# A decoder layer on one core: experts taken in order of their load, the emptier half multiplied in two passes

## The chip, the cores and the metric

The program runs on one core of a Trainium2 chip. The metric is the device time of one execution in microseconds (us), from the first to the last instruction on that core and what the runtime puts around it. Lower is better.

## What is computed

One layer of a decoder trunk on 512 tokens of 1024 channels in float32: three parallel token mixers (dilated attention, gated linear attention, sparse attention), merged and projected; then cross-attention into a memory of 256 tokens; then a mixture of 32 experts, four for each token. Each sublayer ends in `LN(alpha * x + y)`. The change touches the mixture alone:

```python
logits = t @ w_router + b_router                       # t: 512 x 1024
top_logits, top_idx = lax.top_k(logits, TOP_K)         # 4 of 32
gates = jax.nn.softmax(top_logits)
...
gu = xb @ w_gu[e] + b_gu[e]                            # 1024 -> 2048, rows xb of expert e
gate = jnp.minimum(gu[:, :D_FF], 7.0)
up = jnp.clip(gu[:, D_FF:], -7.0, 7.0)
y = ((up + 1.0) * gate * jax.nn.sigmoid(1.702 * gate)) @ w_down[e] + b_down[e]
```

Every expert has 3 x 1024 x 1024 float32 weights, 12.6 MB; all 32 are 402.7 MB. 2048 (token, expert) pairs are spread over 32 experts, 64 each in the mean. With the reference's own inputs the router gives the experts between 46 and 90 tokens; experts 0 and 1 have 70 and 49; of the other 30, in order of load, the first fourteen have 90 to 62 and the last sixteen 61 to 46.

## The kernel before

The mixers and the cross-attention take the first half of the span. Products are made in split precision: a float32 operand is written as hi + lo (`hilo`, lines 82 to 85: ACT rounds hi to float32r, DVE subtracts lo = src - hi), and a product is the sum of three float32r products, hi hi + lo hi + hi lo.

Routing (`route_tile`, `route`) puts each token's place in its expert's list into `posm`, its row number and gate into `V`, and the number of tokens of each expert into `cnt`. `slots` (four experts at a time) turns these into row numbers `GI` and gates `GT` of 96 slots (`RB`) an expert: DVE compares `iota` with `posm` into `Pe` (line 1146), PE multiplies `Pe` with `V`.

The mixture (`moe`, lines 1220 to 1334) goes through the experts 0 to 31. For each one:

- `gather`: POOL fetches up to 96 rows of x into `xg` by an indirect DMA (line 1337); PE transposes them (line 80), ACT and DVE write hi and lo into `xgT`.
- `gate`, `up`, `down`: each is one `product` of 1024 x 1024 weights. SP loads the weights in four chunks of 1 MB (`mraw`, line 1215; twelve buffers in turn), ACT writes `mhi` (line 84), DVE writes `mlo` (line 85; three buffers of each). PE holds 128 x 96 of X and streams 512 columns of a chunk past it, twelve matmuls a chunk: X hi with `mhi`, X lo with `mhi`, X hi with `mlo` (lines 1233 to 1236). Two short matmuls add the biases from `Be`.
- After `gate`: DVE takes min(g, 7) out of PSUM (line 1253), ACT the tanh (line 1254), DVE (t + 1) g (line 1255).
- After `up`: DVE clamps half a row of u out of PSUM (line 1264) and multiplies, (u + 1) g (line 1265), twice. PE transposes g, and `hT` gets hi and lo as `xgT` does.
- After `down`: ACT scales by the gates (line 1276), POOL adds the rows to `y_scratch` in DRAM by an indirect DMA (line 1342).

The program's order is gate(e+1), down(e), gather(e+2), up(e+1); a scheduler of the framework then fixes the order on every engine when the program is built. Each engine works its own list strictly in order. The last expert's `down_last` goes by halves of its columns, and LN3 (`finish`) follows from SBUF. Experts with over 96 tokens would go through a loop behind the end (`more_blocks`), which is not entered where the counts fit.

```python
for x, y in ((0, hi), (1, hi), (0, lo)):                                  # 1233
    for k in range(2):
        for h in range(2):
            self.mm(P[:, h], X[x][:, a * 2 + k], y[:, k, h * 512:h * 512 + 512], ...)
...
nc.vector.scalar_tensor_tensor(g, t, 1.0, g, op0=ALU.add, op1=ALU.mult)    # 1255
```

Of the kernel before, what the change touches and what calls it, by code (L numbers as in the profile page):

```python
# [36 lines left out]
def const_arrays():  # L37
    """Masks and identities: functions of the shapes alone."""
# [24 lines left out]
class K:  # L63
# [177 lines left out]
    def p0(self):  # L241
        """x -> LN0 -> x0 (spilled) and h^T as hi/lo."""
# [280 lines left out]
    def gla_head(self, h, U, lev, ng, bp, bq):  # L523
# [27 lines left out]
        # within-chunk scores, by halves of ever smaller blocks, so that every exponent is <= 0  # L551
# [24 lines left out]
        # across chunks  # L576
# [216 lines left out]
    def gates_steps(self, br, n, n0=0):  # L793
        """The first 2n gate blocks of a branch, kept for its merge in places that the branches' outputs leave free."""
# [12 lines left out]
    def merge_steps(self, br, w_br, Y):  # L807
        """merged^T += 2 sigmoid(m_g)^T * (w_br^T y^T); Y: pairs (hi, lo) of [128, 2, S]."""
# [26 lines left out]
    def w_halves(self, w_dram, pool):  # L835
        """[1024, 1024] as hi/lo tiles [128, 4, 512], indexed [half][k // 4]."""
# [15 lines left out]
    def proj_ln(self, W, X, R, g, b, after, order, late):  # L852
        """R[i] (residual) <- LN(alpha R[i] + X^T W) g + b, tile by tile; after(i) follows each."""
# [25 lines left out]
    def mix_out(self, x1p, xT):  # L879
        """w_o_mix and LN1: x1 in x1p, its transpose in xT."""  # L880
# [35 lines left out]
    def xattn(self, R, xh, xT, ap, x2_done, before_xo):  # L916
# [11 lines left out]
        for c in range(4):  # L928
            # in float32 itself: the tensor engine has time here, the others have not
# [76 lines left out]
        w = I["w_xo"][0]  # L1006
        W = [[self.chunk(w[a * 512:a * 512 + 512, h * 512:h * 512 + 512], h and a) for a in range(2)] for h in range(2)]
# [212 lines left out]
    def moe(self, wk, xgp):  # L1220
# [91 lines left out]
        def scatter(e, o):  # L1312
            self.scatter_rows(o, self.GI[:, e:e + 1])
# [338 lines left out]
```

## Time and profile before

| what | value |
|---|---|
| median of 3 runs (lowest, highest) | 2460.72 us (2459.5, 2465.01) |
| span of the profiled execution | 2459.6 us; the fastest run is 2459.5 us, so the profiler's execution stands for the runs |
| PE, DVE, ACT, POOL busy over the span | 2347.8, 1875.0, 1381.1, 313.4 us (95, 76, 56, 13%) |
| DMA | 531.04 MB, mean 216 GB/s; 340 to 373 GB/s in most of the mixture's slices |
| mixture | from about 1225 us to the end |

The 40 slices of the page are 61.5 us each; the mixture fills the last twenty. A busy PE is not a PE at its peak, since the matmuls are pipelined; that is why durations below are taken from the distance between instructions where that matters. Idle time of an engine counts only where another engine waits for it.

### The profile page before, as it was taken

To read this page: it belongs to the slowest core of one execution; us is meant where nothing else is said; L and a number is where in the kernel's file an instruction comes from. 1 tells how busy PE (TensorE), PEld (TensorE's weight loads), DVE (VectorE), ACT (ScalarE), POOL (GpSimd) and SP (SyncE) were. 2 spreads that over 40 slices of the span, in tenths; PEclk is the share of its full clock that TensorE was granted. 3 is DMA by queue.
4 is the path that set the end of the run, shared out by engine and by line. 5 is a ranking of instruction groups with operands and counts; after the bars stand their busy time and mean duration, and the time that the engine had idled before them with its cause. 6 is when DMAs were issued, how large, how long until landed. Compare 5 with 4: busy or idle time off the path is not lost. (4 is left out here: it accounts for less than half of the span.)

```text
span 2459.6 us, 30893 instructions
## 1 busy us (share of the span) xinstructions
PE 2347.8 (95%) x11491; PEld 1800.1 (73%) x11491; DVE 1875.0 (76%) x2745; ACT 1381.1 (56%) x1709; POOL 313.4 (13%) x287
## 2 busy tenths in 40 slices
PE   7999899999999998999899999999999999999995
PEld 6778789878877776887767767767676676676663
DVE  6465567446678674636689989989898889999997
ACT  3444434345566663134167767777676776767773
POOL 2000233111000002002110110110101101102002
PEclk9999899999999999999699999999999999999997
DMA  8432222332221204225689999999999999999992
GB/s 258 112 81 77 64 56 74 96 96 69 69 65 39 66 21 157 84 86 158 235 301 359 359 332 359 350 340 366 323 370 326 345 343 346 361 351 373 353 328 87
DMA packets 259931, 531.04 MB, mean 216 GB/s; under 512 B 32185, under 2 KB 145046, under 8 KB 259648
## 3 DMA queue, kind: packets, MB, share of 16 engines
q1 hardware_dynamic: 244720, 487.89, 57.2%
q0 software_dynamic: 13040, 33.73, 5.4%
q10 hardware_dynamic: 2016, 7.41, 0.8%
q8 instruction: 92, 1.51, 0.2%
q14 instruction: 63, 0.52, 0.1%
HBM read 509.98 MB, written 22.02 MB: 216 GB/s over the span
## 5 line engine op out<-in xcount | busy, mean ns | idle before, releaser
L85 DVE TENSOR_TENSOR mlo<-mraw,mhi 128x2048 fp32r<-128x2048 f32 x384 | 874.1, 2286 | 102.8 <-ACT mhi L84 98.5
L84 ACT ACTIVATE mhi<-mraw 128x2048 fp32r<-128x2048 f32 x387 | 734.4, 1916 | 233.2 <-PE pd L77 180.6
L77 PE MATMUL pd<-mhi,xgT 128*96 128x512 f32 x2080 | 531.9, 396 | 2.6 <-ACT mhi L84 2.2
L77 PEld LDWEIGHTS pd<-mhi,xgT 128*96 128x96 f32 x2080 | 334.6, 162 | 145.6 <-ACT mhi L84 2.7
L77 PE MATMUL pd<-hT,whi 128*128 128x512 f32 (+1 forms) x1136 | 299.3, 408 | 9.7 <-DVE qs L318 4.3
L77 PE MATMUL pd<-mlo,xgT 128*96 128x512 f32 x1040 | 285.9, 396 | 0.1
L77 PE MATMUL pd<-mhi,hT 128*96 128x512 f32 x992 | 266.9, 405 | 14.4 <-DVE hT L85 11.8
L77 PEld LDWEIGHTS pd<-hT,whi 128*128 128x128 f32 (+1 forms) x1136 | 214.9, 193 | 59.9 <-issue 3.9
L85 DVE TENSOR_TENSOR wlo<-raw,whi 128x1024 fp32r<-128x1024 f32 (+1 forms) x121 | 155.6, 1288 | 125.8 <-ACT whi L84 57.8
L84 ACT ACTIVATE whi<-raw 128x1024 fp32r<-128x1024 f32 (+1 forms) x121 | 127.3, 1058 | 185.7 <-PE pd L77 145.2
L77 PEld LDWEIGHTS pd<-mlo,xgT 128*96 128x96 f32 x1040 | 165.3, 161 | 73.2 <-DVE mlo L85 4.5
L77 PEld LDWEIGHTS pd<-mhi,hT 128*96 128x96 f32 x992 | 157.2, 165 | 78.4 <-DVE hT L85 13.6
L1337 POOL DMA_INDIRECT xg<-x_scratch,GI x31 | 71.5, 2308 | 676.9 <-PE pt L80 599.9
L77 PE MATMUL pd<-hT,wlo 128*128 128x512 f32 (+1 forms) x568 | 156.7, 401 | 0.0
L77 PE MATMUL pd<-mlo,hT 128*96 128x512 f32 x496 | 141.1, 407 | 0.0
L77 PEld LDWEIGHTS pd<-hT,wlo 128*128 128x128 f32 (+1 forms) x568 | 104.9, 188 | 22.8 <-issue 0.7
L85 DVE TENSOR_TENSOR ptl<-pt,pth 128x512 fp32r<-128x512 f32 (+4 forms) x144 | 84.6, 606 | 42.7 <-ACT pth L84 41.7
L84 ACT ACTIVATE pth<-pt 128x512 fp32r<-128x512 f32 (+4 forms) x144 | 72.4, 527 | 68.6 <-PE pt L80 67.6
L77 PEld LDWEIGHTS pd<-mlo,hT 128*96 128x96 f32 x496 | 80.2, 167 | 33.4 <-DVE mlo L85 1.5
L1342 POOL DMA_INDIRECT y_scratch<-o,GI x32 | 59.4, 1858 | 329.0 <-ACT o L1276 254.6
L739 ACT ACTIVATE cz<-cz,c_mn 128x128 f32<-128x128 f32 (+3 forms) x128 | 71.1, 556 | 50.8 <-DVE c_mn L737 50.0
L737 DVE CUSTOM_DVE_ANT_0 cz<-ps,m_full 128x128 f32<-128x128 f32 (+3 forms) x128 | 59.9, 486 | 42.2 <-PE ps L77 33.3
(402 smaller groups left out, 3320.0 us busy)
## 6 DMA issues: line engine op xcount, KB each, us to landing
mraw<-in_w_gu_dram SPq DMA_DIRECT2D x256, 1024.0 KB, 8.4
mraw<-in_w_down_dram SPq DMA_DIRECT2D x128, 1024.0 KB, 6.8
raw<-in_w_in_dram SPq DMA_DIRECT2D x78, 512.0 KB, 4.1
kd<-kd POOLq DMA_DIRECT2D x20, 256.0 KB, 4.1
raw<-in_w_xk_dram SPq DMA_DIRECT2D x8, 512.0 KB, 10.2
raw<-in_w_in_dram SPq DMA_DIRECT2D x16, 256.0 KB, 3.5
raw<-in_w_br_b_dram SPq DMA_DIRECT2D x8, 512.0 KB, 4.1
raw<-in_w_br_c_dram SPq DMA_DIRECT2D x8, 512.0 KB, 4.5
```

The lines of the kernel that those rows point to most:

```text
L77: self.nc.tensor.matmul(out, l, r, start=start, stop=stop)
L84: self.nc.scalar.activation(hi, src, AF.Copy)
L85: (eng or self.nc.vector).tensor_tensor(lo, src, hi.bitcast(F32), op=ALU.subtract)
L737: nc.vector.tensor_tensor_reduce(z[:, :n], P[:, :n], self.m_full[:, 512 - n:], -0.125, 1e30, op0=ALU.add, op1=ALU.min, accum_out=mn[:, h, ...
L739: nc.scalar.activation(z[:, :n], z[:, :n], AF.Exp, bias=mn[:, h, k - 1:k], scale=-1.0, accum_out=den[:, h, k - 1:k])
L1337: self.nc.gpsimd.indirect_dma_start(out=xg, out_offset=None, in_=self.x2d, in_offset=bass.IndirectOffsetOnAxis(ap=self.GI[:, e:e + 1], axi ...
L1342: self.nc.gpsimd.indirect_dma_start(out=self.y2d, out_offset=bass.IndirectOffsetOnAxis(ap=GI, axis=0), in_=o, in_offset=None, bounds_check ...
```

## The change

Behind the routing the experts are put in order of their load on the chip (`turns_of`: a key from `cnt`, its rank, a permutation matrix `one`; `posm` and the gates are permuted by PE, the biases' selector `OH` is built from `one`). Experts 0 and 1 keep the first two turns. Of the other 30 turns the fourteen fullest experts are "wide" (96 slots, three passes as before) and the sixteen emptier ones "narrow": 64 slots, the hi rows and the lo rows side by side as 128 columns of one stationary tile, so that a chunk takes eight matmuls, (hi | lo) with `mhi` and (hi | lo) with `mlo`. The two halves of the result stand in PSUM rows 0 to 63 and 64 to 127: `whole` lets ACT copy the lower half to `u1`, and DVE adds. The turns go wide, wide, and then narrow and wide in turn, with a narrow one last. Which expert's weights a turn loads is read into a register of SP from the table `eix` (30 loads of a register), and the weights' DMAs take their address from it.

Beside that: the first chunk of a narrow expert's gate product is multiplied as plain float32 without splitting (`NDIRECT`); the 1 of (u + 1) goes into the biases; (t + 1) g, (u + 1) g and the clamps of the narrow ones go from DVE to POOL, for the wide experts too; the last expert's sum goes to DRAM only where the loop behind the end is entered.

```diff
+RB, RS = 96, 64
+N_WIDE = 16
+NDIRECT = 1
...
     def bias(self, P, e, j):
-        self.mm(P, self.OH[:, j // 3, e:e + 1].to_broadcast([128, RB]), self.B[:, j % 3 * 512:j % 3 * 512 + 512], False, True)
+        l = self.OH[:, j // 3, e:e + 1].to_broadcast([128, RB if WIDE[e] else 128])
+        self.mm(P, l, self.B[:, j % 3 * 512:j % 3 * 512 + 512], False, True)
...
+        def who(e):
+            if e < 2:
+                return slice(e, e + 1)
+            if len(first) <= e - 2:
+                first.append(nc.sync.value_load(self.eix[0:1, e:e + 1], min_val=0, max_val=31))
+            return bass.ds(first[e - 2], 1)
...
             for a in range(4):
-                hi, lo = self.chunk(w[e, a * 256:a * 256 + 256, c0:c0 + 1024], eng=...)
-                for x, y in ((0, hi), (1, hi), (0, lo)):
+                src = w[who(e), a * 256:a * 256 + 256, c0:c0 + 1024]
+                if not WIDE[e] and bc == 0 and a < NDIRECT:
+                    y = self.chunk_raw(src).rearrange("p (k n) -> p k n", n=1024)
+                    terms = ((X[2].bitcast(F32), y),)
+                else:
+                    hi, lo = self.chunk(src, eng=nc.gpsimd if e == 0 and bc == 0 and a < 3 else None)
+                    terms = ((X[0], hi), (X[1], hi), (X[0], lo)) if WIDE[e] else ((X[2], hi), (X[2], lo))
+                for x, y in terms:
...
+        def whole(P, c, **kw):
+            u = wk.tile([RS, 512], F32, name="u1", tag="u1", bufs=1)
+            nc.scalar.activation(u, P[RS:128, c], AF.Copy, **kw)
+            return u
...
         def gate(e):
-            nc.vector.tensor_scalar(g, P, 7.0, None, op0=ALU.min)
+            if WIDE[e]:
+                nc.vector.tensor_scalar(g, P, 7.0, None, op0=ALU.min)
+            else:
+                for h in range(2):
+                    c = slice(h * 512, h * 512 + 512)
+                    nc.vector.tensor_tensor(g[:, c], P[:RS, c], whole(P, c), op=ALU.add)
+                nc.gpsimd.tensor_scalar(g, g, 7.0, None, op0=ALU.min)
             nc.scalar.activation(t, g, AF.Tanh, scale=0.851)
-            nc.vector.scalar_tensor_tensor(g, t, 1.0, g, op0=ALU.add, op1=ALU.mult)
+            nc.gpsimd.tensor_scalar(t, t, 1.0, None, op0=ALU.add)
+            nc.gpsimd.tensor_tensor(g, t, g, op=ALU.mult)
...
         def up(e):
-                nc.vector.tensor_scalar(u, P[:, c], -7.0, 7.0, op0=ALU.max, op1=ALU.min)
-                nc.vector.scalar_tensor_tensor(g[:, c], u, 1.0, g[:, c], op0=ALU.add, op1=ALU.mult)
+                if WIDE[e]:
+                    nc.vector.tensor_scalar(u, P[:, c], -6.0, 8.0, op0=ALU.max, op1=ALU.min)
+                else:
+                    nc.vector.tensor_tensor(u, P[:RS, c], whole(P, c), op=ALU.add)
+                    nc.gpsimd.tensor_scalar(u, u, -6.0, 8.0, op0=ALU.max, op1=ALU.min)
+                nc.gpsimd.tensor_tensor(g[:, c], u, g[:, c], op=ALU.mult)
...
         def down(e):
-                nc.scalar.activation(o[:, c], P[:, c], AF.Copy, scale=self.GT[:, e:e + 1])
+                if WIDE[e]:
+                    nc.scalar.activation(o[:, c], P[:, c], AF.Copy, scale=gt)
+                else:
+                    u = whole(P, c, scale=self.GT[RS:128, e:e + 1])
+                    nc.vector.scalar_tensor_tensor(o[:, c], P[:RS, c], gt, u, op0=ALU.mult, op1=ALU.add)
...
         def down_last(e, A, PT, gb):
-                    for x, y in ((0, wh), (1, wh), (0, wl)):
+                    for j, y in enumerate(self.chunk(w[who(e), a * 512:a * 512 + 512, cs[h]])):
```

What stands in the engines' lists in the middle of the mixture. DVE, behind an up product, before (`mlo` is line 85's subtraction, `u` and `g` the two operands of the activation):

```order
L1264 TENSOR_SCALAR u<-pd 96x512
L85 TENSOR_TENSOR mlo<-mraw_15952,mhi 128x2048
L1265 SCALAR_TENSOR_TENSOR g<-u,g 96x512
L85 TENSOR_TENSOR mlo<-mraw_15970,mhi 128x2048
L1264 TENSOR_SCALAR u<-pd 96x512
L85 TENSOR_TENSOR mlo<-mraw_15996,mhi 128x2048
L1265 SCALAR_TENSOR_TENSOR g<-u,g 96x512
```

And with the change, behind the up product of a wide expert and then the gate product of a narrow one (line numbers of the changed kernel; its line 116 is the old line 85):

```order
L1407 TENSOR_SCALAR u<-pd 96x512
L116 TENSOR_TENSOR mlo<-mraw_14696,mhi 128x2048
L1407 TENSOR_SCALAR u<-pd 96x512
L116 TENSOR_TENSOR mlo<-mraw_14724,mhi 128x2048
L116 TENSOR_TENSOR mlo<-mraw_14742,mhi 128x2048
L116 TENSOR_TENSOR mlo<-mraw_14760,mhi 128x2048
L116 TENSOR_TENSOR hT<-pt,hT 128x384
L1392 TENSOR_TENSOR g_10798<-pd,u_14713 64x512
L116 TENSOR_TENSOR hT<-pt,hT 128x384
L1392 TENSOR_TENSOR g_10798<-pd,u_14716 64x512
L116 TENSOR_TENSOR mlo<-mraw_14778,mhi 128x2048
```

The multiplications by g are gone from DVE's list; the second half of `u`, which has one buffer, now stands behind a reader on POOL. POOL's list there before, indirect DMAs alone (`xg` the gathered rows, `y_scratch` the sum):

```order
L1337 DMA xg_10753<-x_scratch,GI 96x1024
L1337 DMA xg_10070<-x_scratch,GI 96x1024
L1342 DMA y_scratch<-o,GI 512x1024
L1337 DMA xg_10753<-x_scratch,GI 96x1024
L1342 DMA y_scratch<-o,GI 512x1024
```

POOL with the change, for a narrow and a wide expert:

```order
L1411 TENSOR_TENSOR g_10799<-u,g_10799 96x512 x2
L1393 TENSOR_SCALAR g_10798<-g_10798 64x1024
L1395 TENSOR_SCALAR t<-t 64x1024
L1396 TENSOR_TENSOR g_10798<-t,g_10798 64x1024
L1500 DMA xg_10070<-x_scratch,GI 96x1024
L1505 DMA y_scratch<-o,GI 512x1024
L1410 TENSOR_SCALAR u<-u 64x512
L1411 TENSOR_TENSOR g_10798<-u,g_10798 64x512
L1410 TENSOR_SCALAR u<-u 64x512
L1395 TENSOR_SCALAR t<-t 96x1024
L1411 TENSOR_TENSOR g_10798<-u,g_10798 64x512
L1396 TENSOR_TENSOR g_10799<-t,g_10799 96x1024
```

Between its two indirect DMAs an expert POOL now has four arithmetic instructions (wide) or seven (narrow), in one list with them, where it had none.

## Rows read from the trace of the kernel before

**Rows 1.** Stretches of one expert: engines busy, granted clock, DMA share, GB/s

```profile
2066.30:2102.57 36.27, 36.27 (x168) 25.28 (x167) 33.31 (x23) 25.15 (x19) 3.59 (x2) 1.00 1.01 377
2102.57:2138.84 36.27, 36.27 (x167) 25.29 (x166) 33.37 (x23) 26.06 (x20) 3.45 (x2) 1.00 0.97 355
```

**Rows 2.** Groups of instructions, 1300 to 2400 us: busy, mean ns, idle time before

```profile
L85 DVE TENSOR_TENSOR mlo<-mraw,mhi 128x2048 fp32r<-128x2048 f32 x355 | 808.2, 2286 | 83.4 <-ACT mhi L84 81.6 <-issue 0.4
L84 ACT ACTIVATE mhi<-mraw 128x2048 fp32r<-128x2048 f32 x355 | 673.4, 1916 | 189.7 <-PE pd L77 154.1 <-DMA mraw<-in_w_gu_dram 16.9 <-issue 12.8
...
L1264 DVE TENSOR_SCALAR u<-pd 96x512 f32<-96x512 f32 x59 | 40.3, 683 | 3.7 <-PE pd L77 2.9
L1265 DVE SCALAR_TENSOR_TENSOR g<-u,g 96x512 f32<-96x512 f32 x59 | 40.2, 681 | 0.0
L1255 DVE SCALAR_TENSOR_TENSOR g<-t,g 96x1024 f32<-96x1024 f32 x30 | 36.4, 1214 | 0.0
L1253 DVE TENSOR_SCALAR g<-pd 96x1024 f32<-96x1024 f32 x30 | 36.4, 1213 | 4.8 <-PE pd L77 4.8
```

**Rows 3.** ACT's longest wait, 1300 to 2400 us

```profile
ACT mhi L84 <- PE pd L77: 154.1, 177, 1.9
```

**Rows 4.** Waits in SP's queue, 1300 to 2400 us

```profile
SPq L1215 <- DVE mlo L85: 877.6, 327, 7.5
```

**Rows 5.** PE in order of time: start, us, instruction

```profile
1506.57 2.02 PE L77 MATMUL pd<-mhi,xgT 128*96 128x512 f32 x8
...
1509.35 2.02 PE L77 MATMUL pd<-mhi,xgT 128*96 128x512 f32 x8
```

**Rows 6.** Plain float32 product, groups of 1000 to 1400 us

```profile
L77 PE MATMUL pd<-raw,memT 128*128 128x256 f32 x128 | 29.0, 381 | 0.3 <-DMA raw<-in_w_xv_dram 0.2
```

**Rows 7.** Line 1254, once for each expert: min/median/max ns, first and last start

```profile
L1254 ACT ACTIVATE t<-g x30: 1037/1044/1051, 1311.5 to 2389.9; 96x1024 f32<-96x1024 f32 x30
```

**Rows 8.** POOL, groups of the whole span

```profile
L1309 POOL TENSOR_TENSOR o<-oh,oh 96x1024 f32<-96x1024 f32 x1 | 2.4, 2353 | 6.7 <-DVE oh L1299 6.7
```

**Rows 9.** Line 831 on POOL: min/median/max ns, first and last start

```profile
L831 POOL TENSOR_TENSOR mg<-mg,y x8: 1265/2135/2270, 929.9 to 965.1; 128x512 f32<-128x512 f32 x8
```

**Rows 10.** Line 1299 on DVE, likewise

```profile
L1299 DVE SCALAR_TENSOR_TENSOR oh<-pd,GT,oh x2: 741/744/747, 2424.6 to 2429.7; 96x512 fp32r<-96x512 f32 x2
```

**Rows 11.** DVE, groups of 100 to 1000 us

```profile
L85 DVE TENSOR_TENSOR ptl<-pt,pth 128x256 fp32r<-128x256 f32 x20 | 8.2, 420 | 11.3 <-ACT pth L84 11.1
```

**Rows 12.** DVE around 942 us, in order of time

```profile
941.94 1.22 DVE L85 TENSOR_TENSOR wlo<-raw,whi 128x1024 fp32r<-128x1024 f32 x1
943.08 2.31 DVE L85 TENSOR_TENSOR wl<-raw,wh 128x1024 fp32r<-128x1024 f32 x1
```

**Rows 13.** POOL around 942 us

```profile
942.17 2.14 POOL L831 TENSOR_TENSOR mg<-mg,y 128x512 f32<-128x512 f32 x1 [3.49 <-DVE y L830]
```

**Rows 14.** DVE around 512 us

```profile
512.56 6.95 DVE L85 TENSOR_TENSOR wlo<-raw,whi 128x1024 fp32r<-128x1024 f32 x1 [0.69 <-PE pd L77]
```

**Rows 15.** POOL around 512 us

```profile
512.81 5.61 POOL L661 TENSOR_TENSOR X<-T,pe 128x248 f32<-128x248 f32 x8
```

**Rows 16.** POOL around 228 us

```profile
228.14 0.90 POOL L483 CAST lev<-gE 128x512 uint8<-128x512 f32 x1
...
235.01 0.61 POOL L483 CAST lev<-gE 128x512 uint8<-128x512 f32 x1 [5.13 <-DMA gE<-in_m_lev_dram]
```

**Rows 17.** DVE around 228 us

```profile
227.35 1.22 DVE L85 TENSOR_TENSOR wlo<-raw,whi 128x1024 fp32r<-128x1024 f32 x1
```

**Rows 18.** DVE beside L1309, which runs from 2430.56

```profile
2431.59 1.26 DVE L1305 TENSOR_TENSOR mraw<-mraw,pt 128x512 f32<-128x512 f32 x2
```

**Rows 19.** A register loaded by SP, line 1424: ns, start

```profile
L1424 SPq TENSOR_LOAD <-nxi x1: 477/477/477, 2192.8 to 2192.8; - x1
```

**Rows 20.** A stretch at the mixture's start, columns as in rows 1

```profile
1190.00:1195.00 5.00, 5.00 (x25) 5.00 (x25) 3.82 (x24) 0.30 (x2) 0.00 (x0) 0.50 1.02 415
```

More of the change, by code (lines that the diff above doesn't have):

```diff
@@ L15, with turns @@
 S, D, NT, KT = 512, 1024, 4, 8
-RB = 96
-NX = 24
+RB, RS = 96, 64
+N_WIDE = 16
+NX = 32
+NDIRECT = 1
+def turns():
+    wide, narrow = list(range(2, N_WIDE)), list(range(N_WIDE, 32))
+    o = [0, 1]
+    while wide or narrow:
+        if narrow:
+            o.append(narrow.pop(0))
+        if wide:
+            o.append(wide.pop(0))
+    if o[-1] != 31:
+        o.remove(31)
+        o.append(31)
+    return o, [r < N_WIDE for r in o]
+TURN, WIDE = turns()
 ALPHA = 2.0 ** 0.25
@@ L55, in const_arrays @@
     c["tok"] = p[:, None] + 128 * np.arange(4)[None, :]
+    e = np.arange(32)
+    c["turns"] = np.broadcast_to(np.stack([np.array(TURN), np.where(e < 2, (2 - e) * 2 ** 20, 31 - e),
+                                           np.where(WIDE, 1.0, 0.5)])[None], (128, 3, 32))
+    c["cap"] = np.broadcast_to(np.where(WIDE, RB, RS)[None], (128, 32))
+    c["own"] = p[:, None] % 32 == e[None, :]
     c = {k: np.ascontiguousarray(v, np.float32) for k, v in c.items()}
@@ L1005, in xattn @@
         nc.scalar.dma_start(b, self.bcast(I["ln2_b"][0], D))
-        w = I["w_xo"][0]
-        W = [[self.chunk(w[a * 512:a * 512 + 512, h * 512:h * 512 + 512], h and a) for a in range(2)] for h in range(2)]
+        w = I["w_xo"]
+        W = [[self.chunk(w[:, a * 512:a * 512 + 512, h * 512:h * 512 + 512], h and a) for a in range(2)] for h in range(2)]
         self.moe_biases()
@@ new lines, in route @@
+        nc.vector.tensor_copy(pg[:, :, 0:32], self.posm)
+        nc.vector.tensor_reduce(pg[:, :, 32:64], G.rearrange("p t k e -> p t e k"), op=ALU.add, axis=AX.X)
+        T = self.pt.tile([128, NT, 128], F32, name="pt", tag="pt")
+        for t in range(NT):
+            self.tr(T[:64, t], pg[:, t])
+        pgT = w[:64, 4:8]
+        nc.scalar.activation(pgT, T[:64], AF.Copy)
+        P = self.ps.tile([128, NT, 128], F32, name="ps", tag="ps")
+        for t in range(NT):
+            for j in range(2):
+                self.mm(P[:, t, j * 32:j * 32 + 32], pgT[:, t], self.perm[:, j], True, True)
@@ L1139, in slots, with x_tiles, hl_views @@
+    def x_tiles(self, wide=True):
+        return self.hl_views(self.mp.tile([128, 2 * KT * RB], F32R, name="xgT", tag="xgT", bufs=2), wide)
+    def hl_views(self, t, wide):
+        if wide:
+            t = t.rearrange("p (j k c) -> p j k c", j=2, c=RB)
+            return [t[:, 0], t[:, 1]]
+        t = t[:, :KT * 128].rearrange("p (k c) -> p k c", c=128)
+        return [t[:, :, 0:RS], t[:, :, RS:128], t]
     def slots(self, e0, n, sc):
@@ L1172, in moe_setup @@
         nc.gpsimd.memset(self.OH.bitcast(F32), 0.0)
-        for p in range(4):
-            nc.gpsimd.tensor_copy(self.OH[p * 32:p * 32 + 32, p // 2], self.ident[0:32, 0:32])
         self.B = mp.tile([128, 3 * D // 2], F32R, name="Be")
@@ L1183, in moe_biases @@
         nc.gpsimd.dma_start(r[64:96, 512:1536], I["b_down"][0])
+        for p, c in ((0, D), (64, 0)):
+            nc.gpsimd.tensor_scalar(r[p:p + 32, c:c + 512], r[p:p + 32, c:c + 512], 1.0, None, op0=ALU.add)
         for p, c, n, f in ((0, 0, 1536, 1.0), (64, 0, 512, 1.0), (64, 512, 1024, 2.0)):
@@ L1307, in down_last @@
             self.finish(A, bn, gb)
-            o = wk.tile([RB, D], F32, name="o", tag="o", bufs=1)
-            nc.gpsimd.tensor_tensor(o, hi.bitcast(F32), lo.bitcast(F32), op=ALU.add)
-            return o
         def scatter(e, o):
-            self.scatter_rows(o, self.GI[:, e:e + 1])
+            self.scatter_rows(o, self.GI[:o.shape[0], e:e + 1])
         gate(0)
@@ L1325, in moe @@
             else:
-                scatter(e, down_last(e, *self.finish_first(wk)))
+                down_last(e, *self.finish_first(wk))
             if e + 2 < NE:
@@ L1334, in moe, with scatter_last @@
                 up(e + 1)
+    def scatter_last(self, wk):
+        nc = self.nc
+        hi, lo = [self.last.bitcast(F32)[:, j * D:j * D + D] for j in range(2)]
+        u = wk.tile([RS, D], F32, name="u1")
+        x = wk.tile([128, D], F32, name="ol")
+        nc.vector.tensor_tensor(x, hi, lo, op=ALU.add)
+        nc.scalar.activation(u, x[RS:128], AF.Copy)
+        o = wk.tile([RS, D], F32, name="o")
+        nc.vector.tensor_tensor(o, x[0:RS], u, op=ALU.add)
+        self.scatter_rows(o, self.GI[:RS, 31:32])
     def gather_rows(self, xg, e):
-        self.nc.gpsimd.indirect_dma_start(out=xg, out_offset=None, in_=self.x2d,
-                                          in_offset=bass.IndirectOffsetOnAxis(ap=self.GI[:, e:e + 1], axis=0),
+        n = RB if WIDE[e] else RS
+        self.nc.gpsimd.indirect_dma_start(out=xg[:n], out_offset=None, in_=self.x2d,
+                                          in_offset=bass.IndirectOffsetOnAxis(ap=self.GI[:n, e:e + 1], axis=0),
                                           bounds_check=S - 1, oob_is_err=False)
```

158 lines of the change are left out of this document (110 added, 48 removed).

## The prediction

> **What bounds the kernel now.** I read the windows first. In a stretch of one expert PE is busy for all 36.27 us at full granted clock, while DVE has 33.3 us of work, ACT 25 to 26 and POOL 3.5 [rows 1]. So PE sets the pace, with DVE 3 us behind it. The waits say the same: ACT's `mhi` waits 154.1 us, in 177 cases, for PE to give a weight buffer back [rows 3], and DVE's `mlo` has little idle time of its own [rows 2]. The timeline of PE gives the price of a matmul: twelve of them, one chunk, start 2.78 us after the twelve before, 0.232 us each [rows 5]. SP's queue waits 877.6 us, 327 times, for DVE to free a raw buffer [rows 4]: the weights are not what is late, the buffers are. The tanh of line 1254 runs once an expert, and from its first to its last start there are 29 periods in 1078.4 us, 37.19 us each [rows 7]. So an expert costs 36.27 us and, spread over all, 0.9 us for the steps of `slots`. A pair of experts costs 74.4 us. The program of the change is fifteen pairs of a narrow and a wide expert, with one wide ahead and one narrow behind, so I price one pair and multiply by 15.
>
> **PE.** A narrow chunk has eight matmuls for twelve: 1.85 us. A narrow expert has eleven of those, one direct chunk, biases and transposes. The direct chunk is four plain float32 products of 512 columns; the trace has such a product only with 256 columns, 381 ns a record and two records for each written product [rows 6], so at most 4 x 4 x 0.381 = 6.1 us, at least what it replaces, 1.85 us; I take 3.6 us, between them. With 2.7 us for the rest (36.27 less 12 x 2.78 is 2.9) the narrow expert needs 11 x 1.85 + 3.6 + 2.7 = 26.7 us and the pair 36.3 + 26.7 = 63 us. PE gives 11 us of 74 away and is no longer the bound.
>
> **DVE.** A pair has 33.31 + 33.37 = 66.7 us of it [rows 1]. Out go two multiplications by (t + 1) (1.214 us each) and four by (u + 1) (0.681 each) [rows 2], and one `mlo` of 2.286 for the direct chunk: 2.43 + 2.72 + 2.29 = 7.4 us. The min of the narrow gate (1.213) is replaced by two additions out of PSUM, which I price like the `u` of line 1264, 0.683 each; the two narrow clamps by two additions, at no change: +0.15. The lo rows of narrow `hT` and `xgT` are 256 wide and cost about 0.42 [rows 11] for 0.55: -0.5 over four. New are two weighted sums into `o`, like line 1299 at 0.741 [rows 10]: +1.5. In all 66.7 - 6.3 = 60.4 us a pair. By this alone DVE would do as PE does, 60 to 63 us, and the kernel would be much faster.
>
> **POOL, and what it does to DVE.** POOL's list had no arithmetic. A wide expert now has (t + 1) over 1024 columns, the product over 1024 and two products over 512; a narrow one has these, a min over 1024 and two clamps over 512. Rows nearest to them: two inputs, 1024 columns, 2.353 us [rows 8]; two inputs, 512 columns, 1.27 us where undisturbed [rows 9]; one input, 512 columns, 0.61 [rows 16], so 1.2 for 1024. Wide: 1.2 + 2.35 + 2.54 = 6.1. Narrow: 2.4 + 2.35 + 1.22 + 2.54 = 8.5. Together 14.6 us (13 if 64 rows are a little cheaper, 17 if the rows misprice). POOL has the time: 14.6 + 7 us of 74.
>
> But POOL and DVE do not run beside each other. At 941.94 a DVE subtraction of two SBUF operands runs 1.22 us, the next one, the same shape, takes 2.31 [rows 12]; POOL's addition, which starts at 942.17 and takes 2.14 for 1.27 [rows 13], first waits for the one and then holds up the other. At 512.56 a subtraction of the same shape takes 6.95 us [rows 14]: eight POOL instructions, 5.61 us, go through while it stands [rows 15]. One-input POOL instructions are no exception: the CAST at 228.14 takes 0.90 beside a DVE subtraction [rows 17] and 0.61 alone [rows 16]. DVE instructions that read PSUM do go on: line 1305 keeps its 0.63 us beside POOL's L1309 [rows 18]. The `mlo`, 23 of them in a pair, 52.6 of DVE's 60.4 us, all have two SBUF operands. So nearly each us of POOL arithmetic is a us in which DVE stands. Following the two lists of a pair by hand, in the order shown above, I find most POOL instructions released while an `mlo` heads DVE's list; 0.4 to 3.4 us fall beside a reader of PSUM, and I take 1.5.
>
> **The sum.** A pair on DVE: 60.4 + 14.6 - 1.5 = 73.5; the steps of `slots` add 1.8 as now, and the heads of its list that wait for PE (4.8 and 3.7 us over 30 experts [rows 2]) 0.6: 75.9 us against 74.4. That is +1.5 a pair, +23 over fifteen. ACT gets six copies of 512 columns a pair for two outputs that it loses, under 3 us on an engine with 52 of 74 us taken: nothing. Weights: 30 register loads of 0.48 us on SP [rows 19], some 0.7 us with the two instructions behind it; SP stands idle behind DVE most of the time [rows 4] and twelve buffers lie ahead, so I count 2 us (bounds 0 and 24). The sorting ahead of the mixture is some twenty small DVE and PE steps in a row: +3 (1 to 8; it lies partly beside the weights' first loads). The last expert's `down_last` has a third fewer matmuls, 16 x 0.232 = 3.7, of which I take 2 off. Sum of these: +3. The profiled execution has a span of 2459.6 us, within 0.05% of the median of 2460.7. Forecast: 2460.7 + 23 + 3 = **2486 us**. With POOL at 13 and 3.4 beside PSUM readers a pair takes 72.4 (2434 us); with 17 and 0.4 it takes 79.4 (2539 us).
>
> **Rivals.**
> - *POOL finds room (faster).* DVE's readers of PSUM are some 10 us of a pair, and POOL has long waits between its products; if its list drifts so that it works beside those, up to 8 us of the 14.6 are hidden. The pair then falls to 68 to 72, where the weights come in: 25.2 MB a pair take 67 us at the 377 GB/s of one stretch, 71 at 355 [rows 1], 61 at the 415 of a deep queue [rows 20]. At 71 a pair the time is 2461 - 51 + 3 = 2413 us (2370 to 2450). For it: POOL waits for nothing else, so each of its instructions can move by several us. Against it: its instructions are released by DVE or ACT results at fixed places of DVE's list, and `mlo` stands behind nearly all of them.
> - *A tie.* The pair comes to 74.1 to 74.7; within 5 us of now. It is no mechanism of its own, only what lies between.
> - *POOL is kept out, and the chain up, product, transposes, `hT` becomes the bound (slower still).* Where DVE wins again and again, as POOL did at 512.56 [rows 14, 15], the product waits for the four `mlo` behind the second `u` (9.1 us). `hT` stands right behind those, and DVE then waits for POOL's two products (2.5), eight transposes and ACT's `hT`, some 3 us more than the sum has, in each expert: pair 82, 2460.7 + 114 + 3 = 2578 us. It decides from the point at which POOL's products start after the fourth `mlo`. Against it: at 942.17 POOL waited for one DVE instruction only [rows 13]. The Trainium skill ("SBUF — State Buffer", section "Who interferes with whom") says that a DVE instruction with two SBUF inputs and a GpSimd instruction that reads SBUF contend for a port pair, and that whichever is second to issue blocks until the first is finished. By that rule POOL waits for one `mlo` at most, this rival would have no chance and the forecast what it has; the row at 512.56, where DVE stood first and was kept out over eight instructions, does not agree with it.
> - *The change does not do what it says*: a narrow expert over 64 tokens, and the loop behind the end is entered. The counts, 61 at most among the emptier sixteen and 90 among the others, exclude it unless the sorting differs from them.
>
> **How the numbers follow.** A measurement of this kernel tells about 0.2%, 5 us, from no change. The likeliest case, DVE paced by POOL, holds 0.52 with 2434 to 2539; its part below 2456 is 0.08 and falls to faster, its slow part 0.44. POOL finds room 0.30. The tie, from the ends of both, 0.10. The long chain 0.06, the loop 0.02. So faster 0.38, same 0.10, slower 0.52. The range reaches from 2395, half of the first rival's span, to 2545, the forecast's own end; outside lie the rest of that rival and the last two, under 0.2.
>
> **What would show it.** Right: the mean `mlo` rises from 2286 ns to about 2.8 us (52.6 + 13 over 23), DVE is busy through nearly the whole mixture, PE's busy share there falls to some 83%, the period of the tanh line is 38 us in the mean, ACT's waits for PE are gone, and POOL's products take longer than 2.35 and 1.27. Wrong, to the fast side: `mlo` below 2.6 us and a period under 36.5. Wrong, to the slow side: DVE idle at `hT` behind ACT or PE, or SP's loads in front of late weights with `mhi` waiting for DMA.

## The result, and the profile after

The changed kernel takes 2622.44 us in the median (2617.75 to 2627.53) where the kernel before, run beside it, takes 2462.86: a ratio of 1.0645 [1.0622, 1.0668], 160 us slower. The forecast was 2486, with 2395 to 2545.

The line of the tanh is now 1394; where [rows 7] had 29 periods of 37.19 us, here are its 30 starts behind the first pair:

```profile
L1394 ACT ACTIVATE t<-g x30: 1038/1044/1063, 1336.1 to 2564.8; 64x1024 f32<-64x1024 f32 x16, 96x1024 f32<-96x1024 f32 x14
```

That is 42.4 us an expert. From the third start to the thirty-first the periods alternate between some 32 and 52 us, 83.8 us a pair in the mean, where the forecast had 75.9 and the kernel before 74.4. The third start itself stands at 1336.1 for 1311.5: 25 us are lost ahead of the mixture's steady part. From the third start to the last it is 1228.7 us for 1078.4, 150 more; behind the last start, in the shorter `down_last` and what follows it, 55.4 us for 69.7, 14 less. These three make up the 160. The window of one pair, with the columns of [rows 1], says that no engine is full:

```profile
1726.00:1810.00 84.00, 69.29 (x300) 50.75 (x299) 67.61 (x60) 53.62 (x42) 45.62 (x15) 0.92 0.91 320
```

PE has 69 us of 84, DVE 68, ACT 54, POOL 46. The forecast wanted DVE busy through nearly all of it. The groups of 1300 to 2500 us (columns of [rows 2]; 116 is the old line 85; `...` marks lines left out) show which instructions became long:

```profile
L116 DVE TENSOR_TENSOR mlo<-mraw,mhi 128x2048 fp32r<-128x2048 f32 x329 | 789.8, 2429 | 151.2 <-ACT mhi L115 149.4 <-PE pd L108 1.5
...
L1410 POOL TENSOR_SCALAR u<-u 64x512 f32<-64x512 f32 x28 | 143.2, 5113 | 149.6 <-DVE u L1409 149.6
L1411 POOL TENSOR_TENSOR g<-u,g 96x512 f32<-96x512 f32 x30 | 141.8, 4726 | 29.9 <-DVE u L1407 29.1 <-DVE tab L1575 0.8
...
L1411 POOL TENSOR_TENSOR g<-u,g 64x512 f32<-64x512 f32 x28 | 61.6, 2202 | 1.3
...
L1393 POOL TENSOR_SCALAR g<-g 64x1024 f32<-64x1024 f32 x14 | 38.9, 2781 | 57.3 <-DVE g L1392 47.8 <-DVE tab L1585 9.4
...
L1396 POOL TENSOR_TENSOR g<-t,g 96x1024 f32<-96x1024 f32 x14 | 33.2, 2369 | 0.1
```

`mlo` takes 2.43 us for 2.29, 0.14 more, which is 47 us over all 329. POOL's clamp of 64 x 512 takes 5.11 us (1.91 at the shortest) and its product of 96 x 512 takes 4.73, where 1.27 was the undisturbed price [rows 9]. DVE was held up a little by POOL; POOL was held up far more by DVE. The longest waits of the same stretch (engine, line and what it waited for; total, times, longest) say who paid:

```profile
ACT mhi L115 <- PE pd L108: 185.3, 166, 3.9
...
PE pt L111 <- POOL g L1411: 154.7, 41, 6.3
...
DVE mlo L116 <- ACT mhi L115: 149.4, 99, 4.2
...
PE pd L108 <- DVE hT L116: 37.3, 14, 5.2
...
DVE u L1409 <- POOL g L1411: 29.5, 14, 3.2
...
DVE u L1407 <- POOL g L1411: 26.6, 15, 2.7
```

PE's transposes of g wait 154.7 us for POOL, 41 times, a wait that did not exist before, and ACT's `mhi` waits for PE as it did [rows 3]. DVE in its turn waits 29.5 + 26.6 us for POOL, at the one buffer of `u` that POOL's product has to read first. One instance in order of time, first DVE, then POOL, then PE (start, duration):

```profile
1732.61 6.68 DVE L116 TENSOR_TENSOR mlo<-mraw,mhi 128x2048 fp32r<-128x2048 f32 x3
1739.21 0.55 DVE L116 TENSOR_TENSOR hT<-pt,hT 128x384 fp32r<-128x384 f32 x1
```

```profile
1732.77 7.65 POOL L1411 TENSOR_TENSOR g<-u,g 96x512 f32<-96x512 f32 x1 [0.80 <-DVE u L1407]
1742.97 2.79 POOL L1393 TENSOR_SCALAR g<-g 64x1024 f32<-64x1024 f32 x1 [2.56 <-DVE g L1392]
```

```profile
1735.24 0.61 PE L108 MATMUL pd<-Be,OHe 128*128 128x512 f32 x2
1740.47 0.55 PE L111 MATMUL pt<-ident,g 96*128 96x96 f32 x4 [4.61 <-POOL g L1411]
1740.80 3.51 PE L108 MATMUL pd<-mhi,hT 128*96 128x512 f32 x8
...
1747.99 2.03 PE L108 MATMUL pd<-mhi,hT 128*96 128x512 f32 x8
```

POOL's product starts at 1732.77 and ends at 1740.42: three `mlo` in a row, 6.68 us, go through while it stands, and it ends 1.1 us behind them. The same product takes the same 7.65 us in 13 pairs of 1300 to 2500 us, each time 0.15 us behind the start of the first of three `mlo`. PE has nothing left from 1735.9 on and waits 4.61 us for the transposes. The eight matmuls behind that wait take 3.51 us, eight of the same shape later 2.03: the granted clock of this pair is 0.92 in the mean where it was 1.00 [rows 1], and behind this wait it is 0.53, near the lower of its two levels, 1.2 GHz of 2.4:

```profile
1740.80:1744.30 3.50, 3.50 (x12) 2.36 (x11) 1.24 (x2) 1.09 (x2) 1.33 (x1) 0.53 1.03 418
```

The next row of POOL runs while DVE has no instruction at all (DVE is through at 1742.88 and starts the next at 1746.29): a min over 64 x 1024 takes 2.79 us by itself. The forecast had 1.2.

SP's queue, 1200 to 2500 us, with the register loads of line 1341 (ns, first and last start):

```profile
SPq L1315 <- DVE mlo L116: 756.7, 268, 11.0
...
SPq L1341 <- DVE eix L1211: 37.5, 1, 37.5
```

```profile
L1341 SPq TENSOR_LOAD <-eix x30: 262/263/483, 1228.2 to 1247.3; - x30
```

SP waits 37.5 us for the table of turns, and then the 30 loads run from 1228.2 to 1247.3, in one bunch. Behind that its waits are for buffers, as in [rows 4].

### The profile page after: what moved, and what is told of

Read it like the earlier page. It is cut to its first block, busy times and chain, and to the rows that moved or that the text cites. A ratio compares the mean times of both kernels' runs of the same rounds, so it can differ in the third digit from the quotient of the medians.

```text
span 2620.2 us, 30555 instructions
## 1 busy us (share of the span) xinstructions
PE 2281.5 (87%) x10747; PEld 1774.9 (68%) x10747; DVE 1850.7 (71%) x2702; ACT 1385.9 (53%) x1758; POOL 942.2 (36%) x465
## 5 line engine op out<-in xcount | busy, mean ns | idle before, releaser
L108 PE MATMUL pd<-mhi,xgT 128*96 128x512 f32 (+1 forms) x1488 | 401.7, 408 | 3.4 <-DVE xgT L116 2.2
L108 PEld LDWEIGHTS pd<-mhi,xgT 128*96 128x96 f32 (+1 forms) x1488 | 253.9, 173 | 100.9 <-issue 11.4
L108 PE MATMUL pd<-mlo,xgT 128*96 128x512 f32 (+1 forms) x976 | 275.1, 404 | 15.5 <-DVE mlo L116 15.5
L108 PE MATMUL pd<-mhi,hT 128*96 128x512 f32 (+1 forms) x752 | 239.0, 461 | 37.6 <-DVE hT L116 37.3
L1411 POOL TENSOR_TENSOR g<-u,g 96x512 f32<-96x512 f32 (+1 forms) x64 | 221.1, 3455 | 39.6 <-DVE u L1407 37.2
L108 PEld LDWEIGHTS pd<-mlo,xgT 128*96 128x96 f32 (+1 forms) x976 | 169.9, 177 | 75.1 <-DVE mlo L116 22.1
L108 PEld LDWEIGHTS pd<-mhi,hT 128*96 128x96 f32 (+1 forms) x752 | 150.0, 205 | 95.3 <-DVE hT L116 41.1
L1410 POOL TENSOR_SCALAR u<-u 64x512 f32<-64x512 f32 x32 | 159.2, 4974 | 152.7 <-DVE u L1409 152.6
L108 PE MATMUL pd<-mlo,hT 128*96 128x512 f32 (+1 forms) x496 | 152.4, 434 | 0.0
L1395 POOL TENSOR_SCALAR t<-t 96x1024 f32<-96x1024 f32 (+1 forms) x32 | 106.2, 3320 | 56.4 <-ACT t L1394 55.3
```

Source lines behind the costliest of these rows:

```text
L108: self.nc.tensor.matmul(out, l, r, start=start, stop=stop)
L1395: nc.gpsimd.tensor_scalar(t, t, 1.0, None, op0=ALU.add)
L1410: nc.gpsimd.tensor_scalar(u, u, -6.0, 8.0, op0=ALU.max, op1=ALU.min)
L1411: nc.gpsimd.tensor_tensor(g[:, c], u, g[:, c], op=ALU.mult)
```

## The experiments

Theory P: POOL's instructions, held back by DVE, are what PE waits for. Theory R: the two passes themselves, the sorting or the register loads cost the time. In all short diffs below, `+` is what the experiment has.

**The multiplications on DVE** (e1), the rest of the change kept:

```diff
-nc.gpsimd.tensor_scalar(g, g, 7.0, ...)          # narrow; the clamps of u likewise
+nc.vector.tensor_scalar(g, g, 7.0, ...)
-nc.gpsimd.tensor_scalar(t, t, 1.0, ...); nc.gpsimd.tensor_tensor(g, t, g, op=ALU.mult)
+nc.vector.scalar_tensor_tensor(g, t, 1.0, g, op0=ALU.add, op1=ALU.mult)
-nc.gpsimd.tensor_tensor(g[:, c], u, g[:, c], op=ALU.mult)
+nc.vector.tensor_tensor(g[:, c], u, g[:, c], op=ALU.mult)
```

> The whole change, but the min, the clamps and the products by g on DVE in place of POOL. Theory P (POOL's instructions, shut out while mlo runs, are what PE's transposes wait for): the wait of the transposes for g goes, DVE paces a pair at 60.4 + 5.2 + 2.4 + 1.8 = 70 us (68 to 72) where it is 83.8, so 2385 to 2440 us, faster than the kernel before. Theory R (the two passes themselves, their copy and addition through one buffer, the register loads and the sorting cost the time): pair above 80, over 2560 us.

2524.05 us, 1.0244 [1.0222, 1.0266] of the kernel before, between the ranges of the two theories. POOL's part is 98 of the 160 us. But 60 us stay, where theory P alone wanted the kernel to be faster than before. The window of a pair:

```profile
1726.00:1803.00 77.00, 67.77 (x299) 49.35 (x297) 69.75 (x71) 52.52 (x42) 11.16 (x4) 0.96 0.95 340
```

DVE has 69.75 us of work, just what the sum gave (70), yet the pair takes 77, 77.6 in the mean. PE and DVE wait for each other within it, and the transposes wait 22.3 us in all, for DVE (1300 to 2400 us):

```profile
ACT mhi L115 <- PE pd L108: 247.6, 189, 4.5
...
DVE mlo L116 <- ACT mhi L115: 113.2, 126, 2.3
...
PE pd L108 <- DVE hT L116: 86.2, 28, 3.7
...
PE pt L111 <- DVE g L1410: 22.3, 14, 1.6
```

**Only POOL's products, in the kernel before** (e3), the 1 of (u + 1) in the biases as in the change:

```diff
-nc.vector.scalar_tensor_tensor(g, t, 1.0, g, op0=ALU.add, op1=ALU.mult)
+nc.gpsimd.tensor_scalar(t, t, 1.0, None, op0=ALU.add)
+nc.gpsimd.tensor_tensor(g, t, g, op=ALU.mult)
-nc.vector.tensor_scalar(u, P[:, c], -7.0, 7.0, op0=ALU.max, op1=ALU.min)
-nc.vector.scalar_tensor_tensor(g[:, c], u, 1.0, g[:, c], op0=ALU.add, op1=ALU.mult)
+nc.vector.tensor_scalar(u, P[:, c], -6.0, 8.0, op0=ALU.max, op1=ALU.min)
+nc.gpsimd.tensor_tensor(g[:, c], u, g[:, c], op=ALU.mult)
```

> The kernel before, with nothing of the change but (t + 1) g and (u + 1) g on POOL (the 1 of (u + 1) in the biases). Theory P: PE waits for POOL's products before each hT as in the changed kernel, 4 to 7 us an expert, so 2580 to 2680 us. Theory R: DVE has 2.6 us less of 33.3 and PE paces as before, 2455 to 2490 us.

2535.55 us, 1.0290 [1.0259, 1.0321]: slower by 70, short of the 115 that theory P wanted at least and far from theory R. In the kernel that has no narrow expert, no sorting and no second pass, the same instructions become long (POOL, 1300 to 2400 us):

```profile
L1268 POOL TENSOR_TENSOR g<-u,g 96x512 f32<-96x512 f32 x56 | 203.1, 3627 | 213.8 <-DVE u L1267 213.8
L1257 POOL TENSOR_SCALAR t<-t 96x1024 f32<-96x1024 f32 x28 | 112.3, 4010 | 127.0 <-ACT t L1256 126.9
```

But PE's wait for POOL is short here, and DVE is held up as well (same stretch):

```profile
L85 DVE TENSOR_TENSOR mlo<-mraw,mhi 128x2048 fp32r<-128x2048 f32 x332 | 817.9, 2487 | 76.3 <-ACT mhi L84 75.9
```

```profile
DVE u L1267 <- POOL g L1268: 32.1, 27, 1.2
...
PE pd L77 <- DVE mlo L85: 29.2, 39, 2.3
...
PE pt L80 <- POOL g L1268: 24.9, 27, 3.6
```

`mlo` takes 2.49 us for 2.29, 67 us over all 332, and DVE waits 32 us more at `u`; PE's transposes wait 25 us for POOL, its weight products 29 us for `mlo`. So the two engines shut each other out in both directions, and where all experts are wide part of POOL's cost comes by DVE, which theory P left out. How the 70 us divide was not separated.

**All experts but the last wide**, with the multiplications on DVE (e4, from e1) and on POOL (e2, from the change):

```diff
-N_WIDE = 16
+N_WIDE = 31
```

> The changed kernel with 96 slots and three passes for all experts but the last, and the multiplications on DVE: the kernel before with sorting, permuted tables and register loads. Both theories on POOL: 2465 to 2490 us, that is 37.2 us an expert, some 25 us more ahead of the third expert, less a cheaper tail. If the register loads cost time at each turn: over 2500 us.

2473.36 us, 1.0042 [1.0025, 1.0059]. The sorting, the permuted tables and the register loads cost some 10 us of the 160: the third tanh starts at 1322.8 for 1311.5, and an expert without `slots` takes the same 36.1 us as before. (The last turn, which is narrow, takes 9 us more, and the end behind it 12 less.)

> The changed kernel with 96 slots and three passes for all experts but the last, POOL's multiplications kept. Theory P: 2590 to 2690 us, as the narrow experts are not what makes POOL late. Theory R: like the run with these on DVE, 2465 to 2490 us.

2534.85 us in one run, 61 more than e4: POOL's cost again, without narrow experts, below the expected 2590 as in e3, and with `mlo` at 2.48 us as there.

So of 160 us some 10 are the sorting, 98 POOL's list, and 50 lie in the two passes, which e1 has and e4 has not. The next four runs start from e1 and look at these 50. Theory B: DVE is behind in the narrow stretches, and what it has to spare in the wide ones does not carry over. Theory C: PE waits for the long chain from a narrow up product to hT, whatever DVE's load.

**Three direct chunks** (e5):

```diff
-NDIRECT = 1
+NDIRECT = 3
```

> The run with the multiplications on DVE (2524 us), with three of the four chunks of a narrow gate product as plain float32 in place of one. Theory B (DVE, at 2.29 us a chunk, is behind in the narrow stretches, and what it gains in the wide ones does not carry over): two mlo less a pair, DVE's 4.6 us, against some 2 x 1.5 us more on PE; 2 to 4.6 us a pair, 2455 to 2495 us. Theory C (the long chain from a narrow up product through copy, addition, clamp and product to hT is what PE waits for, whatever DVE's load): PE's longer products add to it, 2510 to 2570 us.

2511.15 us, 1.0204 [1.0181, 1.0228]: outside B's range, at the lower end of C's, and the pair is as long as with one (77.7). 4.6 us less on DVE a pair bought nothing there while the turns alternate; the 13 us under e1 lie ahead of the third tanh, in the last turn and behind it. Theory B as I put it, with DVE's load alone, misses here.

**Four buffers of `mhi` and `mlo`** (e6), paid for with two of the twelve raw buffers:

```diff
-        return self.hlp.tile([128, 2048], F32R, name=n, tag=n, bufs=3)
+        return self.hlp.tile([128, 2048], F32R, name=n, tag=n, bufs=4)
-self.raw_pool(ctx.enter_context(self.pool("mraw0", side="right")), 2)
+self.raw_pool(ctx.enter_context(self.pool("mraw0", side="right")), 1)
-self.raw_pool(self.ctx.enter_context(self.pool("mraw1", side="right")), 5)
+self.raw_pool(self.ctx.enter_context(self.pool("mraw1", side="right")), 4)
```

> The same run with four buffers of mhi and of mlo in place of three, paid for with two of the twelve raw buffers. Theory B: another chunk of ready weights is carried from wide into narrow stretches, 2 to 6 us a pair, 2435 to 2495 us. Theory C: 2510 to 2535 us. If the two raw buffers are missed (mhi waiting for DMA): above 2535.

2488.93 us, 1.0117 [1.0086, 1.0149], 35 us less than e1 although it has fewer raw buffers: within B's range.

**Two buffers of `u` and `u1`** (e8), paid for with one raw buffer:

```diff
-u = wk.tile([RS, 512], F32, name="u1", tag="u1", bufs=1)
+u = wk.tile([RS, 512], F32, name="u1", tag="u1", bufs=2)
-u = wk.tile([128, 512], F32, name="u", tag="u", bufs=1)[:n]
+u = wk.tile([128, 512], F32, name="u", tag="u", bufs=2)[:n]
-self.raw_pool(pc.enter_context(self.pool("mraw3")), 2)
+self.raw_pool(pc.enter_context(self.pool("mraw3")), 1)
```

> The same run with two buffers of u and of the copy u1 in place of one, paid for with one raw buffer. Theory C: the two halves of a narrow product overlap, ACT's wait for the addition (40 us) goes and hT comes 1 to 3 us sooner, 2470 to 2505 us. Theory B: DVE has no less to do, 2515 to 2535 us.

2515.56 us, 1.0225 [1.0200, 1.0251], pair 77.5: outside C's range, at the lower end of B's. The copies' buffers are not it, so theory C's chain is not shortened where I thought.

**The turns grouped** (e7): wide, wide, then fourteen wide, then sixteen narrow.

```diff
-    while wide or narrow:
-        if narrow:
-            o.append(narrow.pop(0))
-        if wide:
-            o.append(wide.pop(0))
+    o += wide + narrow
```

> The same run with the turns in another order: the fourteen wide ones, then the sixteen narrow ones, not in turn. Theory B (nothing is carried over anyway): wide turns at 36 to 37 us as before the change, narrow ones at DVE's 34 to 36, so 2420 to 2460 us, and alternating is what costs. Theory C: narrow turns in a row have the shorter cover, 40 us and more each, 2500 to 2560 us.

2476.67 us, 1.0062 [1.0040, 1.0084]: 47 us less than e1 for the order of the turns alone, though 17 above B's range and far below C's. The wide half and the narrow half:

```profile
1330.00:1800.00 470.00, 461.65 (x2123) 326.08 (x2122) 428.12 (x338) 334.96 (x238) 55.62 (x26) 0.99 0.98 350
1880.00:2400.00 520.00, 425.76 (x1726) 322.69 (x1727) 484.39 (x464) 373.92 (x311) 142.93 (x32) 0.88 0.95 350
```

The wide turns are those of the kernel before (36.1 us without `slots`, 37.5 in the mean). The narrow ones take 36.9 us in the mean, by the starts of the tanh, for B's 34 to 36; PE is busy for 82% of them and DVE for 93%. A narrow turn relieves PE but not DVE: by these shares it has some 34 us of DVE's work, as a wide one has (an estimate). It takes as long as a wide one, and the pair, 74.5 us, is no shorter than the 74.4 of before. PE's longest wait in that half is for DVE's g, where it had been for POOL's:

```profile
PE pt L107 <- DVE g L1406: 88.9, 26, 6.8
```

**Grouped, with three direct chunks** (e9: e7 with the diff of e5), **and with four buffers too** (e10: with that of e6 as well).

> The run with multiplications on DVE and the turns grouped (2477 us, a narrow turn 36.8 us with DVE 93% busy), with three direct chunks in a narrow gate product in place of one. Theory B (DVE paces the narrow turns): DVE has 4.6 us less of 36.8, PE some 3.4 more of 30, so 33 to 34 us a narrow turn, 16 times 3: 2420 to 2440 us, faster than the kernel before. Rival D (the weights pace them: 350 GB/s in the wide and in the narrow stretch alike): no gain, 2468 to 2482 us.

2468.87 us, 1.0022 [1.0006, 1.0038]: theory B missed, the time is that of rival D. Its narrow turns take 36.8 us with neither PE nor DVE full:

```profile
1900.00:2380.00 480.00, 423.90 (x1572) 289.84 (x1571) 395.40 (x402) 296.42 (x259) 44.03 (x29) 0.94 0.98 354
```

So DVE's load, 82% now for 93%, is not by itself what sets a narrow turn. Nor do the engines wait for the weights, as D would have it; these are all such waits of the same 480 us:

```profile
ACT mhi L111 <- DMA mraw<-in_w_gu_dram: 2.9, 2, 1.9
DVE mlo L112 <- DMA mraw<-in_w_gu_dram: 1.7, 2, 1.0
```

> The run before this one, with four buffers of mhi and mlo for three and ten raw buffers for twelve. Theory B: 0 to 1.5 us a narrow turn more, 2395 to 2435 us. Rival D: as with three buffers, within 8 us of that run or slower for the raw buffers.

2442.89 us, 0.9915 [0.9891, 0.9938], in the range of neither B nor D. Of the 26 us under e9 some 12 lie in the wide turns and 7 in the narrow ones, which fall from 36.8 to 36.3; in their stretch no wait for the weights is left, and neither PE nor DVE is full:

```profile
1900.00:2380.00 480.00, 423.83 (x1620) 281.85 (x1619) 401.87 (x403) 304.02 (x270) 58.16 (x28) 0.98 0.99 360
```

Rival D falls by these waits, more than by the half us.

**Grouped with four buffers and one direct chunk** (e14: e7 with the diff of e6), **and the kernel before with four buffers** (e13: that diff alone).

> Multiplications on DVE, grouped turns, one direct chunk, four buffers of mhi and mlo. If DVE's sum paces the narrow turns (93% busy at three buffers): within 10 us of the run with three buffers, 2465 to 2480 us. If the three buffers are what ties DVE to PE within a turn: 2440 to 2460 us.

2441.95 us, 0.9894 [0.9865, 0.9923], faster than both kernels.

```profile
1330.00:1800.00 470.00, 469.04 (x2182) 331.44 (x2181) 434.14 (x344) 334.69 (x243) 72.16 (x26) 1.00 0.99 356
1900.00:2380.00 480.00, 396.80 (x1610) 295.23 (x1609) 452.80 (x427) 349.29 (x294) 62.26 (x30) 0.93 0.99 362
```

Its wide half has PE at 469 of 470 us, and in the narrow half DVE is at 94%. Over e7 the wide turns give some 10 us, the narrow ones 8 (36.4 us each), the last turn 11 (35.1 us for 45.9). The fourth buffer is worth 35 us here and 26 from e9 to e10; two more direct chunks are worth 8 with three buffers (e7 to e9) and nothing with four.

> The kernel before with four buffers of mhi and mlo for three and ten raw buffers for twelve, nothing else. If the two passes carry the gain of the run with grouped turns, three direct chunks and four buffers (2443 us): 2450 to 2466 us here, as PE is busy nearly all the time. If the fourth buffer alone carries it: 2435 to 2447 us.

2469.39 us, 1.0009 [0.9996, 1.0023]. The fourth buffer alone gives the kernel before nothing. The 1.1% of e14 needs both, narrow turns in a row and the fourth buffer. Part of it is the shorter end, which the whole change has: 58.8 us behind the last tanh in e14 for 69.7 before.

**Back to POOL.** The changed kernel with the turns grouped (e11: the diff of e7), with four buffers (e15: that of e6), and with only the products on POOL (e12):

```diff
-nc.gpsimd.tensor_scalar(g, g, 7.0, ...)
+nc.vector.tensor_scalar(g, g, 7.0, ...)
-nc.gpsimd.tensor_scalar(t, t, 1.0, ...)
+nc.vector.tensor_scalar(t, t, 1.0, ...)
-nc.gpsimd.tensor_scalar(u, u, -6.0, 8.0, ...)
+nc.vector.tensor_scalar(u, u, -6.0, 8.0, ...)
```

> The changed kernel as it is, POOL's arithmetic kept, with the turns grouped: wide ones, then narrow ones. Theory P+B (POOL's late products and the alternation each cost their own part): 2622 less about 47, 2560 to 2595 us. If the alternation is what makes POOL late: 2480 to 2520 us. If POOL is worse where two narrow turns follow one another (14 us of its instructions a turn): above 2610.

2549.55 us, 1.0353 [1.0323, 1.0384]. Grouping takes 73 off, more than the 47 expected, and the time is 10 us under the range of P+B; POOL still costs 73 over e7. Of its 98 in the alternating order some 25 come from the two together.

> The changed kernel with POOL doing only the two-operand products, and the min, the clamps and the (t + 1), which have one operand, on DVE. Theory P1 (what counts is POOL's own time on the way to hT, and one-operand instructions take it 2.8 us for 1024 columns): POOL's 21.6 us a pair fall to 9.9, half of the 98 us or more come back, 2540 to 2580 us. Theory P2 (what counts is that products with g wait while mlo run, whatever else POOL does): 2590 to 2625 us.

2566.65 us, 1.0412 [1.0383, 1.0441], in the range of P1: 56 of POOL's 98 us come back by taking the min, the clamps and the additions of 1 away from it, though DVE has them then. The product of 96 x 512 is kept out as before (1300 to 2400 us):

```profile
L1411 POOL TENSOR_TENSOR g<-u,g 96x512 f32<-96x512 f32 x28 | 131.3, 4690 | 25.5 <-DVE u L1407 24.7 <-DVE tab L1575 0.8
```

> The changed kernel as it is, POOL's arithmetic and the alternating turns kept, with four buffers of mhi and mlo for three and ten raw buffers for twelve. If POOL's late products and the alternation are separate costs: 2622 less the 35 that the fourth buffer gave without POOL, 2575 to 2600 us. If more mlo ready in a row only keep POOL out for longer: 2605 us and above. If the fourth buffer covers POOL's lateness too: below 2560.

2614.77 us, 1.0598 [1.0565, 1.0630]: the 35 us that the fourth buffer gave in e6 shrink to 8 here, a time that the second reading wanted: the buffer doesn't cover POOL's lateness. Its trace shows that lateness moved (1300 to 2500 us): the product of 96 x 512 comes sooner, 3.08 us for 4.73, and the min is kept out instead, 6.13 for 2.78.

```profile
L1411 POOL TENSOR_TENSOR g<-u,g 96x512 f32<-96x512 f32 x30 | 92.2, 3075 | 49.5 <-DVE u L1407 46.7 <-DVE tabi L1589 2.8
...
L1393 POOL TENSOR_SCALAR g<-g 64x1024 f32<-64x1024 f32 x15 | 91.9, 6125 | 76.0 <-DVE g L1392 75.7
```

That a longer row of ready `mlo` is what does it was not shown.

## Why the prediction was wrong

- **The side that is held back.** The step "nearly each us of POOL arithmetic is a us in which DVE stands" failed. I took the direction from the row at 512.56, where DVE stands behind eight POOL instructions [rows 14, 15]. In the mixture it is DVE that comes in rows, and it is mainly POOL that stands: `mlo` rose to 2.43 us and not to 2.8, which is 3.3 us over the 23 of a pair where the sum had 13.1 (14.6 - 1.5), while POOL's product took 4.73 us for 1.27. In e3 DVE loses more, 0.2 us in each of an expert's twelve `mlo`, still only a third of POOL's 7.6 us of arithmetic there (by the shortest prices below). What I had as the third rival, POOL kept out and PE starved ahead of `hT`, with 2578 us and a chance of 0.06, is POOL's main part of what happened; the 60 us that stay in e1 are not in it. Its condition was that POOL's products come after the fourth `mlo`; three sufficed, as the row at 1732.77 and its twelve like show. I held [rows 13] against it, where POOL had its turn between two subtractions; what decides between that case and this one the runs don't show. The Trainium skill's rule ("SBUF — State Buffer", sections "Who interferes with whom" and "Summary: rules for kernel authors"), by which whichever is second to issue blocks until the first is finished, let POOL wait for one `mlo`. The trace doesn't agree: 7.65 us over three of them.
- **POOL's prices.** The 0.61 us for one input and 512 columns, "so 1.2 for 1024", was mis-sized: 2.78 us in each of the 14 instructions of line 1393. The row was a CAST to uint8 [rows 16], another operation with another output type. With that price, half of it for a clamp (an estimate; the shortest clamp here took 1.91) and 2.34 and 1.26, the shortest products here, a pair has 3 x 2.78 + 2 x 1.4 + 2 x 2.34 + 4 x 1.26 = 21 us and not 14.6. By e12 these one-operand instructions are worth 56 us, their price and their waits together. On DVE the same min takes 0.685 us (e1), a quarter.
- **The sum over a pair.** "A pair on DVE: 60.4 + ..." counts DVE's work of a narrow and a wide turn together. The work was sized well: 70 by the forecast's own rows for e1, 69.75 measured. But a pair takes DVE's sum only if the two turns can lend each other time. With three buffers they don't: a wide turn is PE's, 36.1 us without `slots`, a narrow one takes 36.9 though PE is busy for 82% of it, and in turn they cost 3 us a pair more than in two groups (77.6 for 74.5). This step hid that a narrow turn saves nothing. DVE has 93% of it in e7, but that DVE sets its length is not shown, since in e9 DVE has 82% and the turn is as long. A depth that matters is that of `mhi` and `mlo`, three, which the sum did not look at; with a fourth the pair takes 75.6 (e6).
- **PE** gave its time away as forecast: a pair has 68 us of it in e1 and 69 here (63 forecast, at the full clock), and PE was no longer the bound. **Sorting and register loads** were put at 5 us and cost 10 (e4). SP's idle time of 37.5 us behind the table is most likely why, as the weights' stream stops there; that was not tried. The end behind the last tanh got 14 us shorter, where I took 2 off.
- What is left open: what paces the narrow turns in e9, where no engine is full. The fourth buffer shortens them a little (e10); which engine's order the third one ties was not tried. The granted clock of the narrow stretches does not settle it: 0.88, 0.94, 0.98 and 0.93 in e7, e9, e10 and e14, with turns of 36.9, 36.8, 36.3 and 36.4 us. Open too: how much of POOL's 98 us comes by the clock (0.92 in the pair shown, 0.96 in e1's), and how much by the one buffer of `u`, since two were tried only with the products on DVE (e8).

## What to carry to other kernels

Two engines that shut each other out are priced by who comes in rows: a single instruction can wait for several of the other's, so a short product on the way to PE doesn't belong on POOL beside back-to-back subtractions on DVE. Sums of engine time over stretches with different bounds did not hold here, since little work carries across three buffers; compare the turns one by one, and try the grouped order. Take a price from the same operation and types, or bound it from both sides: 0.61 and 2.78 us are both "one operand on POOL".

## What the runs showed of the hardware that was not expected

- On POOL these one-operand instructions are dearer than the two-operand ones: 2.78 us for a min over 64 x 1024 float32 (2777 to 2792 ns in 14 instances), 2.34 us for the shortest product over 1024 columns.
- DVE is cheap on the same: 0.685 us for that min and 0.41 us for a clamp of 64 x 512 from SBUF (e1), less than the 0.68 of an instruction that reads as many columns out of PSUM [rows 2].
- The exclusion can hold over a row of instructions, in both directions: DVE behind eight of POOL [rows 14, 15], POOL behind three of DVE (7.65 us for 1.26); and it can change hands after one [rows 12, 13]. What decides is not shown.
